# Up-projections with x's upper and lower halves in one 512-column matmul, and the two sums added on the way out

## The chip, the cores and the metric

The kernel runs on one core of a Trainium2 chip, in one launch. The metric is the device time of a run in microseconds (us), of which the median of three is given.

The engines are named as the profile names them: PE is TensorE's matmul and PEld its weight load, DVE is VectorE, ACT is ScalarE, POOL is GpSimd, SP is SyncE, which here issues the weights' DMAs. Every engine takes its instructions in the order in which they stand in its queue.

## The reference, cut to what matters

A backbone of two layers serves two groups of 128 tokens with the same weights: 256 tokens of 2048 channels. Each layer has a mixer and then a gated feed-forward network (FFN) with a convolution of width 3 over the tokens. The change is in the FFN's up-projection, here `h @ w_up` with 2048 channels in and 2 x 5632 out:

```python
def _conv_ffn(h, w_up, cw, cb, w_down, n_rows):
    bsz, n, _ = h.shape
    up = (h @ w_up).reshape(bsz, n_rows, n // n_rows, 2 * D_FF)
    pad = jnp.pad(up, ((0, 0), (0, 0), (1, 1), (0, 0)))
    conv = pad[:, :, :-2] * cw[0] + pad[:, :, 1:-1] * cw[1] + pad[:, :, 2:] * cw[2] + cb
    gate, val = jnp.split(conv.reshape(bsz, n, 2 * D_FF), 2, axis=-1)
    return (jax.nn.silu(gate) * val) @ w_down
```

All inputs are float32.

## The kernel before, in words

**Products in halves.** Each float32 operand is cut into an upper half (rounded to the matmul's fp32r) and a lower one (the rest). A product is the sum of three: upper x upper, upper weights x lower activations, lower weights x upper activations. Of the activations, `H[:, kt]` holds for each of 16 K-tiles (128 channels) the upper halves of 256 tokens in columns 0 to 255 and the lower halves in columns 256 to 511.

**Weights.** They come in units of 1 MB (`raw`, four buffers) over SP's queue, in the order of their use. Each unit is split in two steps of [128, 1024]: ACT writes the upper halves `wh` (line 149), DVE the lower ones `wl` (line 150). There are three buffers of each, so up to three steps' weights are split ahead; a step's buffer comes free when PE has used it.

**Up-projection.** A group has four output tiles of 128 channels (two of the gate, two of the values) and 16 K-tiles: eight steps of two K-tiles. `t_products` (line 789, matmuls at line 796) runs, for each output tile and K-tile, three matmuls of 256 columns, all three into the same 256 columns of a PSUM bank; two output tiles lie in a bank. A layer has 22 groups. The first (`u_products`, line 805) and the second have their own handling of the norm; the other 20 are what the change touches. Groups take their banks from the pool `acc` (four banks, line 246).

**The way out.** At a group's end (line 1396) ACT copies each bank into a buffer `z` that has a zero beside each row of tokens: one copy of the first 128 tokens of both tiles (line 1408), and one of the rest for each tile (line 1410). Then follow, piece by piece beside the next group's steps, the convolution (`conv`: line 1356 on ACT, 1360 twice on DVE), SiLU on ACT (line 1420), the product of gate and value on POOL (lines 1421 and 1424), and its split into `G` (line 702 on ACT, 703 on DVE), which the down-projection reads. CUTS (16, 16, 12) says after how many of the 44 tiles of the gate a part of the down-projection runs.

**Beside it.** The modulation vectors of later sections are spread over the stages: as units of eight matmul records on PE (line 437), or as sums along rows on DVE (line 456, four instructions a unit, `junk<-rows`). `RATES` sets how many of each go beside a unit of weights. In layer 1's FFN both run out early.

**Order.** The code queues the work in the order told; a scheduler in the recording layer then fixes the order of each engine's queue. Waits between engines are by semaphores.

Of the kernel before, what the change touches and what calls it, by code (L numbers as in the profile page):

```python
# [18 lines left out]
P = 128  # L19
D = 2048  # L20
KD = D // P
T = 256
# [36 lines left out]
# columns of the packed per-channel vectors  # L59
# [7 lines left out]
# where the output projection's 16 K-tiles lie: mixer B's first half, the heads, B's second half  # L67
# [171 lines left out]
def backbone_kernel(ctx: ExitStack, tc: tile.TileContext, a: dict):  # L239
# [6 lines left out]
    acc_pool = ctx.enter_context(tc.tile_pool(name="acc", bufs=ACC_BUFS, space=PSUM))  # L246
# [34 lines left out]
    def g0(i):  # L281
        return held["G0"][:, i]
# [4 lines left out]
    # ---- small inputs and constants  # L287
# [56 lines left out]
    # ---- modulation vectors: two rows of a tile's 32 for each condition and group of channels,  # L344
    # four K-tiles at once
# [13 lines left out]
    def mod_first(kt0, n):  # L359
        """The first norm's shift and scale of n tiles of channels."""  # L360
# [38 lines left out]
    def mod_section(s):  # L399
        """512 channels either through the array, K on partitions, or summed along rows of K."""  # L400
# [112 lines left out]
        # both kinds evenly, the products last  # L513
# [85 lines left out]
    def rsqrt_mean(sums, n, width):  # L599
        """(sums / n + eps) ** -0.5, a Newton step after the square root's table."""  # L600
# [15 lines left out]
    def spread(r):  # L616
        """Each column of r [tokens, n] on 128 columns."""
# [7 lines left out]
    def across(ps, spreads):  # L625
        """The columns as rows, the same on all partitions of ps."""
# [3 lines left out]
    def sum_tokens(x, first, last):  # L630
        """Sums over channels, tokens on partitions."""
# [37 lines left out]
    def put_norm(gain, sec=None, ahead=HL_BUFS):  # L669
        """The next norm's statistics, modulation units filling the gap in the products."""  # L670
# [28 lines left out]
    def split(out, src):  # L699
        """out[:, 0:n] the upper, out[:, n:2n] the lower halves of float32 words."""  # L700
# [25 lines left out]
    def make_folded(kt, shift):  # L726
        """Sum and difference of channels half a group apart, in their places."""
# [7 lines left out]
    def make_u(kt):  # L735
        """h before the norm's factor and the shift."""
# [22 lines left out]
    def pre_u(shift, made):  # L759
        """The statistics under way, then h itself behind the products that don't need it."""  # L760
# [14 lines left out]
    def pre_h(shift, upto=KD, made=None):  # L775
        """h's K-tiles as the first group comes to need them."""
# [28 lines left out]
    def u_products(ps, wh, wl, rhs, kts, first, last):  # L805
        """Like t_products, of the rows before the norm's factor and of the shifts; a bank for a tile."""
# [28 lines left out]
    def put_unit(ap, kt0, first, last, products, rhs, ps, end, pre=None, banks=2):  # L835
        """Four K-tiles of a group of 512 output columns, or two."""
        steps = []
        for half in range(ap.shape[-1] // 1024):
            kts = (kt0 + 2 * half, kt0 + 2 * half + 1)

            def fn(wh, wl, kts=kts):
                if kts[0] == first:
                    ps.clear()
                    ps.extend(acc() for _ in range(banks))
                products(ps, wh, wl, rhs, kts, first, last)
                if kts[1] == last:
                    end(ps)
# [19 lines left out]
    # ================================ layer 0: mixers A and B ================================  # L867
    def put_mixers():
# [18 lines left out]
        def store(out, ps, spill, func, queue=st.bg, front=False):  # L887
            """A group's sums through an activation."""
# [45 lines left out]
        def end_t(name, block, func):  # L934
            """Four channel tiles of a block, through an activation."""
# [28 lines left out]
        def queue_head(pair, hh, pt):  # L964
# [91 lines left out]
                # both directions have the same values to sum  # L1056
# [6 lines left out]
            def states():  # L1063
                """S after a direction's first chunk, and the context's after both."""
# [35 lines left out]
            def outputs():  # L1100
                """Tokens on partitions."""
# [135 lines left out]
        # as K-tiles of h come to be known, the first groups' partial sums  # L1237
# [93 lines left out]
    def open_late():  # L1331
        """Room for what comes after the mixers."""
# [397 lines left out]
```

## Time and profile before

| what | value |
|---|---|
| runs | 2369.51, 2373.82, 2376.21 us; median 2373.82 |
| profiled execution, its own time (first to last instruction: the span) | 2371.5 us |
| mean granted TensorE clock | 0.990 |
| PE, DVE, ACT, POOL busy | 98%, 70%, 49%, 16% of the span |
| HBM read | 584 MB, mean 248 GB/s |

The profiled execution has no time of its own beside the span. An engine's busy share is the union of its instructions; PE's matmuls overlap each other in the records, so a busy PE says nothing of its speed, and the distance between the starts of two matmuls does. Rows of the timeline merge neighbours with the same names: "x2" is two instructions, the time is from the first one's start to the last one's end.

### The profile page before, as it was taken

Reading aid. Unit: us, or ns where it says so; the run is one execution under the profiler, and the core shown is the slowest. Engines: PE = TensorE matmul, PEld = TensorE weight load, DVE = VectorE, ACT = ScalarE, POOL = GpSimd, SP = SyncE. Lnnn points to the kernel's source line nnn. Section 1 sums busy time; section 2 is a strip of 40 time slices with the busy share of each in tenths; the row PEclk is TensorE's granted clock in tenths of the full one; section 3 lists DMA queues with packets and bytes.
Section 4 is the critical chain, followed back from the end, with each engine's and each line's share of the span. In section 5 each row is a group of like instructions: output and inputs, shape, how many; then the busy total and the mean of one; then the engine's idle time right before and its main releaser. Section 6 shows DMA issues by size and latency. Waiting matters only on the chain.

```text
span 2371.5 us, 44833 instructions
## 1 busy us (share of the span) xinstructions
PE 2322.9 (98%) x18584; PEld 2146.4 (91%) x18584; DVE 1649.4 (70%) x2672; ACT 1170.6 (49%) x1812; POOL 373.6 (16%) x417
## 2 busy tenths in 40 slices
PE   6999999999999999999999999999999999999997
PEld 4788878788999999999999997999999999999997
DVE  3558966755777767778677787787885566555665
ACT  5336754544655534455335445546554455534552
POOL 0002321213121100111001142233110011100113
PEclk9999999999999999999999999999999999999998
DMA  8977777788667777777777778764665555555552
GB/s 322 382 311 253 262 247 276 264 313 326 228 220 298 268 289 279 292 277 287 287 288 275 287 267 311 281 213 161 231 217 190 181 179 179 193 179 180 184 176 102
DMA packets 88124, 590.11 MB, mean 249 GB/s; under 512 B 9840, under 2 KB 12272, under 8 KB 20336
## 3 DMA queue, kind: packets, MB, share of 16 engines
q1 hardware_dynamic: 84896, 582.01, 66.9%
q10 hardware_dynamic: 3024, 5.24, 0.6%
q8 instruction: 145, 2.38, 0.4%
q14 instruction: 59, 0.48, 0.1%
HBM read 584.07 MB, written 3.15 MB: 248 GB/s over the span
## 4 chain that ended last, share of the span: by engine, by line
PE 91%; DVE 4%; ACT 1%; DMA 1%; POOL 1%; issue 1%; SPq 0%; DVEq 0%; POOLq 0%; ACTq 0%
PE acc L796 77%; PE modacc L437 4%; PE acc L827 4%; DVE wl L150 1%; PE misc L1047 1%; PE modacc L382 1%; PE acc L812 1%; DVE HS L703 0%; DMA early<-in_mod 0%; DVE junk L482 0%; PE acc L1471 0%; ACT wh L149 0%; PE misc L1112 0%; DMA rows<-in_crow 0%; PE misc L1500 0%
## 5 line engine op out<-in xcount | busy, mean ns | idle before, releaser
L796 PE MATMUL acc<-HS,wh 128*128 128x256 f32 x6656 | 1227.3, 286 | 10.0 <-DVE ush L1374 4.8
L150 DVE TENSOR_TENSOR wl<-raw,wh 128x1024 fp32r<-128x1024 f32 x704 | 874.2, 1248 | 476.9 <-ACT wh L149 473.0
L149 ACT CAST wh<-raw 128x1024 fp32r<-128x1024 f32 x704 | 735.0, 1048 | 824.0 <-PE acc L796 703.5
L796 PEld LDWEIGHTS acc<-HS,wh 128*128 128x128 f32 x6656 | 1038.1, 191 | 67.9 <-issue 46.4
L796 PE MATMUL acc<-HS,wl 128*128 128x256 f32 x3328 | 944.0, 284 | 1.6 <-DVE wl L150 1.6
L796 PE MATMUL acc<-G,wh 128*128 128x256 f32 x3840 | 696.5, 284 | 0.0
L796 PEld LDWEIGHTS acc<-HS,wl 128*128 128x128 f32 x3328 | 638.7, 192 | 3.8 <-DVE wl L150 3.5
L796 PEld LDWEIGHTS acc<-G,wh 128*128 128x128 f32 x3840 | 598.1, 192 | 26.8 <-issue 22.6
L796 PE MATMUL acc<-G,wl 128*128 128x256 f32 x1920 | 543.0, 283 | 0.0
L796 PEld LDWEIGHTS acc<-G,wl 128*128 128x128 f32 x1920 | 368.2, 192 | 0.1
L1421 POOL TENSOR_TENSOR gate<-gate,c 128x128 f32<-128x128 f32 x88 | 86.6, 985 | 1126.5 <-DVE c L1360 1060.4
L456 DVE SCALAR_TENSOR_TENSOR junk<-rows 128x1024 bf16<-128x1024 f32 x176 | 222.0, 1261 | 1.4
L1360 DVE SCALAR_TENSOR_TENSOR c<-z,cw,c 128x258 f32<-128x258 f32 x352 | 171.2, 520 | 19.4 <-ACT c L1356 17.0
L437 PE MATMUL modacc<-raw,cs 128*32 128x512 f32 x832 | 114.9, 613 | 0.9 <-DMA raw<-in_mod 0.9
L1356 ACT ACTIVATE c<-z,cw 128x258 f32<-128x258 f32 x176 | 102.6, 613 | 0.0
L702 ACT CAST G<-gate 128x256 fp32r<-128x256 f32 x88 | 35.8, 407 | 129.2 <-POOL gate L1424 129.2
L827 PE MATMUL acc<-wh,HS 128*128 128x512 f32 x256 | 85.6, 402 | 0.0
L703 DVE TENSOR_TENSOR G<-gate,G 128x256 fp32r<-128x256 f32 x88 | 45.0, 511 | 53.4 <-ACT G L702 53.4
L709 POOL TENSOR_TENSOR h<-X,rstd 128x256 f32<-128x256 f32 x44 | 41.2, 946 | 245.9 <-DVE HS L703 213.1
L1303 DVE SCALAR_TENSOR_TENSOR X<-acc,mods,X 128x128 f32<-128x128 f32 x256 | 69.2, 343 | 14.9 <-PE acc L796 14.9
L593 POOL TENSOR_TENSOR sq<-X 128x256 f32<-128x256 f32 x48 | 53.3, 1110 | 154.7 <-DVE X L1303 144.7
L482 DVE SCALAR_TENSOR_TENSOR junk<-quarter,rows 128x512 bf16<-128x512 f32 x96 | 71.7, 747 | 8.5 <-ACT rows L536 5.2
(195 smaller groups left out, 1428.6 us busy)
## 6 DMA issues: line engine op xcount, KB each, us to landing
raw<-in_up SPq DMA_DIRECT2D x176, 1024.0 KB, 4.9
raw<-in_mod SPq DMA_DIRECT2D x106, 1024.0 KB, 5.3
raw<-in_down SPq DMA_DIRECT2D x88, 1024.0 KB, 4.9
raw<-in_w_in SPq DMA_DIRECT2D x49, 1024.0 KB, 6.8
rows<-in_mod SPq DMA_DIRECT2D x44, 1024.0 KB, 4.9
raw<-in_w_out SPq DMA_DIRECT2D x32, 1024.0 KB, 6.7
early<-in_mod SPq DMA_DIRECT2D x30, 1024.0 KB, 10.1
quarter<-in_modq SPq DMA_DIRECT2D x24, 512.0 KB, 3.6
```

Of the source, the lines that this page charges most:

```text
L149: nc.scalar.copy(out=wh, in_=r)
L150: self.last_split = nc.vector.tensor_tensor(out=wl, in0=r, in1=wh.bitcast(F32), op=ALU.subtract).ins
L437: nc.tensor.matmul(ps[0][32 * j : 32 * j + 32, :], lhsT=cs[:, 4 * u + j, 3 - cg : 35 - cg], rhs=raw[:, 512 * j : 512 * j + 512], start=fir ...
L456: nc.vector.scalar_tensor_tensor(out=junk, in0=raw[:, k], scalar=1.0, in1=late["rows"][:, g, k], op0=ALU.mult, op1=ALU.mult, accum_out=(mo ...
L482: nc.vector.scalar_tensor_tensor(out=junk, in0=raw[:, 512 * i : 512 * i + 512], scalar=1.0, in1=mx["rows"][:, g], op0=ALU.mult, op1=ALU.mu ...
L593: nc.gpsimd.tensor_tensor(out=sq, in0=X[:, t], in1=X[:, t], op=ALU.mult)
L796: nc.tensor.matmul(ps[b][:, jj * T : (jj + 1) * T], lhsT=w[:, i, c], rhs=rhs(kt)[:, xs], start=(kt == first and n == 0 and jj == 0), stop= ...
L827: nc.tensor.matmul(ps[g][:, :], lhsT=rhs(kt)[:, xs], rhs=w[:, i, :], start=(kt == first and n == 0), stop=(kt == last and n == 2),)
L1303: nc.vector.scalar_tensor_tensor(out=X[:, t, s], in0=z, scalar=mods[:, sec, g, t : t + 1], in1=X[:, t, s], op0=ALU.mult, op1=ALU.add,)
L1356: nc.scalar.activation(out=o, in_=z[:, 1:259], func=AF.Identity, scale=tap(w + 1), bias=tap(w + 3))
L1360: nc.vector.scalar_tensor_tensor(out=o, in0=z[:, i : i + 258], scalar=tap(w + i), in1=o, op0=ALU.mult, op1=ALU.add)
L1421: nc.gpsimd.tensor_tensor(out=y[:, 0:P], in0=sg[:, 0:P], in1=cv[j + 2][:, 0:P], op=ALU.mult)
```

## The change

For the 20 groups of each layer from the third on, a group becomes two half-groups, each of two output tiles (one of the gate, and the tile of values that belongs to it) with the whole K. A step now holds four K-tiles of 256 output columns, where it had two K-tiles of 512; the weights in HBM are laid out for it, in units of the same size. For each output tile and K-tile the new `wide_products` runs two matmuls: the upper weights on all 512 columns of `H[:, kt]`, which fills a whole bank, with the two upper-weight sums beside each other, and the lower weights on the upper 256 columns, into the bank's first half. Each output tile has a bank of its own. On the way out, ACT copies the first half's sums into `z` and DVE adds the second half's, for the first 128 tokens and then for the rest. The pool `acc` holds two pairs of banks where it held four banks, and all other users take their two banks as a pair. Convolution, gate and split are the same functions, with the tiles' numbers as arguments.

```diff
-    acc_pool = ctx.enter_context(tc.tile_pool(name="acc", bufs=ACC_BUFS, space=PSUM))
+    acc_pool = ctx.enter_context(tc.tile_pool(name="acc", bufs=ACC_BUFS // 2, space=PSUM))
...
+    def acc_pair():
+
+        return acc_pool.tile([P, 2, 512], F32, tag="acc", name="acc")
+
+    halves = []
+
     def acc():
-        return acc_pool.tile([P, 512], F32, tag="acc", name="acc")
+        if not halves:
+            pair = acc_pair()
+            halves.extend((pair[:, 0], pair[:, 1]))
+        return halves.pop(0)
...
+    def wide_products(ps, wh, wl, rhs, kts, first, last):
+
+
+        wh, wl = (w.rearrange("p k n -> p (k n)").rearrange("p (k n) -> p k n", n=256) for w in (wh, wl))
+        for j in range(2):
+            c = slice(j * P, (j + 1) * P)
+            for i, kt in enumerate(kts):
+                nc.tensor.matmul(
+                    ps[0][:, j], lhsT=wh[:, i, c], rhs=rhs(kt), start=(kt == first), stop=False,
+                    skip_group_check=True,
+                )
+                nc.tensor.matmul(
+                    ps[0][:, j, HI], lhsT=wl[:, i, c], rhs=rhs(kt)[:, HI], start=False, stop=(kt == last),
+                    skip_group_check=True,
+                )
...
+        per = 4 if products is wide_products else 2
         for half in range(ap.shape[-1] // 1024):
-            kts = (kt0 + 2 * half, kt0 + 2 * half + 1)
+            kts = tuple(range(kt0 + per * half, kt0 + per * half + per))
...
+                def end_wide(ps, i, gi=gi, tile0=tile0):
+
+                    st.flush()
+                    z = late["zs"][0]
+                    late["zs"].rotate(-1)
+                    upper, lower = (
+                        ps[0][:, :, s].rearrange("p j (r t) -> p j r t", t=64) for s in (HI, LO)
+                    )
+                    rows = z[:, :, 130:260].rearrange("p j (r t) -> p j r t", t=65)[:, :, :, 0:64]
+                    first = z[:, :, 1:129]
+                    for out, y, l in (
+                        (first, ps[0][:, :, 0:P], ps[0][:, :, T : T + P]),
+                        (rows, upper[:, :, 2:4], lower[:, :, 2:4]),
+                    ):
+                        nc.scalar.copy(out=out, in_=y)
+                        nc.vector.tensor_tensor(out=out, in0=l, in1=out, op=ALU.add)
+                    zs, cv, ft = (z[:, 0], z[:, 1]), {}, tile0 + 2 * gi + i
+                    for f in (
+                        lambda: task(cv, zs, 0, ft),
+                        lambda: task(cv, zs, 1, ft + NFT),
+                        lambda: gate(cv, 2 * gi + i, 0, 1),
+                    ):
+                        st.bg.extend((f, None))
```

**How the orders move.** ACT's queue at a group's end in layer 1, before (z is the buffer with the zeros, c the convolution, wh the upper halves of a step's weights, gate the SiLU, G what the down-projection reads):

```order
L1408 COPY z_5061<-acc 128x2x128
L1410 COPY z_5061<-acc 128x2x64 x2
L1356 ACTIVATE c<-z_5061,cw 128x258
L149 CAST wh<-raw 128x1024
L1408 COPY z_5057<-acc 128x2x128
L1410 COPY z_5057<-acc 128x2x64 x2
L1356 ACTIVATE c<-z_5057,cw 128x258
L1420 ACTIVATE gate<-c 128x258
L1356 ACTIVATE c<-z_5061,cw 128x258
L1356 ACTIVATE c<-z_5057,cw 128x258
L149 CAST wh<-raw 128x1024
```

And now, at a half-group's end in layer 1 (lines 1481, 1385, 1431 and 711 are the copies, the convolution, the SiLU and the cast to G):

```order
L149 CAST wh<-raw 128x1024 x2
L1481 COPY z_5018<-acc 128x2x128
L1481 COPY z_5018<-acc 128x2x2x64
L149 CAST wh<-raw 128x1024
L1385 ACTIVATE c<-z_5018,cw 128x258 x2
L149 CAST wh<-raw 128x1024
L1431 ACTIVATE gate<-c 128x258
L711 CAST G_2299<-gate 128x256
L149 CAST wh<-raw 128x1024 x2
```

The six copies of a group are now two for each half-group, both convolutions stand behind both copies, and the cast to G stands once in four splits.

DVE's queue at a group's end in layer 0, before (wl is a step's lower halves, junk a modulation sum):

```order
L150 TENSOR_TENSOR wl<-raw,wh 128x1024 x3
L1360 SCALAR_TENSOR_TENSOR c<-z_5061,cw,c 128x258 x2
L150 TENSOR_TENSOR wl<-raw,wh 128x1024
L1360 SCALAR_TENSOR_TENSOR c<-z_5057,cw,c 128x258 x2
L1360 SCALAR_TENSOR_TENSOR c<-z_5061,cw,c 128x258
L1360 SCALAR_TENSOR_TENSOR c<-z_5057,cw,c 128x258
L1360 SCALAR_TENSOR_TENSOR c<-z_5061,cw,c 128x258
L1360 SCALAR_TENSOR_TENSOR c<-z_5057,cw,c 128x258
L150 TENSOR_TENSOR wl<-raw,wh 128x1024
L703 TENSOR_TENSOR G_2334<-gate,G_2334 128x256 x2
L150 TENSOR_TENSOR wl<-raw,wh 128x1024
L456 SCALAR_TENSOR_TENSOR junk,mods<-rows 128x1024 x2
```

And now, at a half-group's end in layer 0 with modulation sums (line 1482 is the add, 465 a sum, 1389 the convolution, 712 the split to G):

```order
L150 TENSOR_TENSOR wl<-raw,wh 128x1024
L1482 TENSOR_TENSOR z_5014<-acc,z_5014 128x2x128
L465 SCALAR_TENSOR_TENSOR junk,mods<-rows 128x1024
L1482 TENSOR_TENSOR z_5014<-acc,z_5014 128x2x2x64
L465 SCALAR_TENSOR_TENSOR junk,mods<-rows 128x1024
L1389 SCALAR_TENSOR_TENSOR c<-z_5014,cw,c 128x258 x4
L150 TENSOR_TENSOR wl<-raw,wh 128x1024
L465 SCALAR_TENSOR_TENSOR junk,half<-rows 128x1024
L712 TENSOR_TENSOR G_2299<-gate,G_2299 128x256
L465 SCALAR_TENSOR_TENSOR junk,half<-rows 128x1024
L150 TENSOR_TENSOR wl<-raw,wh 128x1024 x2
```

Before, the two lower halves behind a group's end had only convolutions and the split to G around them; now two adds and up to four sums stand there.

## Rows read from the trace of the kernel before

**Rows 1.** The page, part 1: busy us, share, instructions by engine.

```profile
PE 2322.9 (98%) x18584; PEld 2146.4 (91%) x18584; DVE 1649.4 (70%) x2672; ACT 1170.6 (49%) x1812; POOL 373.6 (16%) x417
```

**Rows 2.** The page, part 4: the chain that ended last, by engine.

```profile
PE 91%; DVE 4%; ACT 1%; DMA 1%; POOL 1%; issue 1%; SPq 0%; DVEq 0%; POOLq 0%; ACTq 0%
```

**Rows 3.** Windows from 659 us: us, busy (x count) by engine, clock, DMA.

```profile
659.00:1120.00 461.00, 460.14 (x3766) 431.28 (x3765) 346.41 (x502) 224.46 (x362) 48.69 (x62) 1.00 0.75 278
1120.00:1590.00 470.00, 467.11 (x3818) 432.88 (x3817) 360.84 (x611) 216.27 (x340) 95.73 (x96) 1.00 0.75 278
1630.00:2360.00 730.00, 727.56 (x6041) 727.18 (x6040) 458.30 (x619) 362.36 (x559) 87.40 (x112) 1.00 0.52 183
```

**Rows 4.** Groups by line and shape: TensorE matmuls that read x's halves.

```profile
L796 PE MATMUL acc<-HS,wh 128*128 128x256 f32 x6656 | 1227.3, 286 | 10.0 <-DVE ush L1374 4.8 <-ACT HS L702 2.3 <-DVE HS L703 2.2
L796 PE MATMUL acc<-HS,wl 128*128 128x256 f32 x3328 | 944.0, 284 | 1.6 <-DVE wl L150 1.6
```

**Rows 5.** Timeline, TensorE, 1961 to 1966: start us, us, what, xcount.

```profile
1961.02 0.40 PE L796 MATMUL acc<-HS,wh 128*128 128x256 f32 x2
...
1965.72 0.41 PE L796 MATMUL acc<-HS,wh 128*128 128x256 f32 x2
```

**Rows 6.** Timeline, TensorE, 156 to 161: matmuls of 512 columns.

```profile
156.54 0.39 PE L827 MATMUL acc<-wl,HS 128*128 128x512 f32 x1
...
160.70 0.39 PE L827 MATMUL acc<-wl,HS 128*128 128x512 f32 x1
```

**Rows 7.** Timeline, TensorE, 189.4 to 190: 512 columns, then 256.

```profile
189.47 0.39 PE L827 MATMUL acc<-wh,HS 128*128 128x512 f32 x1
189.70 0.40 PE L796 MATMUL acc<-HS,wh 128*128 128x256 f32 x2
189.94 0.28 PE L796 MATMUL acc<-HS,wl 128*128 128x256 f32 x1
```

**Rows 8.** Timeline, ScalarE, layer 0: first copy behind a group.

```profile
965.78 0.38 ACT L1408 COPY z<-acc 128x256 f32<-128x256 f32 x1 [0.53 <-PE acc L796]
...
990.10 0.38 ACT L1408 COPY z<-acc 128x256 f32<-128x256 f32 x1 [0.53 <-PE acc L796]
```

**Rows 9.** Timeline, ScalarE, layer 1: first copy behind a group.

```profile
1960.49 0.38 ACT L1408 COPY z<-acc 128x256 f32<-128x256 f32 x1 [0.50 <-PE acc L796]
...
1983.63 0.38 ACT L1408 COPY z<-acc 128x256 f32<-128x256 f32 x1 [0.50 <-PE acc L796]
```

**Rows 10.** Groups by line and shape: busy us, mean ns, idle before.

```profile
L150 DVE TENSOR_TENSOR wl<-raw,wh 128x1024 fp32r<-128x1024 f32 x704 | 874.2, 1248 | 476.9 <-ACT wh L149 473.0 <-PE acc L796 2.1
L149 ACT CAST wh<-raw 128x1024 fp32r<-128x1024 f32 x704 | 735.0, 1048 | 824.0 <-PE acc L796 703.5 <-DMA raw<-in_w_in 36.8 <-DMA raw<-in_w_out 22.1
L456 DVE SCALAR_TENSOR_TENSOR junk<-rows 128x1024 bf16<-128x1024 f32 x176 | 222.0, 1261 | 1.4
L1360 DVE SCALAR_TENSOR_TENSOR c<-z,cw,c 128x258 f32<-128x258 f32 x352 | 171.2, 520 | 19.4 <-ACT c L1356 17.0
L1356 ACT ACTIVATE c<-z,cw 128x258 f32<-128x258 f32 x176 | 102.6, 613 | 0.0
L1421 POOL TENSOR_TENSOR gate<-gate,c 128x128 f32<-128x128 f32 x88 | 86.6, 985 | 1126.5 <-DVE c L1360 1060.4 <-ACT gate L1420 52.2 <-ACT wh L149 13.9
L1424 POOL TENSOR_TENSOR gate<-gate,c 128x128 f32<-128x128 f32 x88 | 57.0, 647 | 0.0
L703 DVE TENSOR_TENSOR G<-gate,G 128x256 fp32r<-128x256 f32 x88 | 45.0, 511 | 53.4 <-ACT G L702 53.4
L1410 ACT COPY z<-acc 128x128 f32<-128x128 f32 x168 | 36.8, 276 | 0.0
L702 ACT CAST G<-gate 128x256 fp32r<-128x256 f32 x88 | 35.8, 407 | 129.2 <-POOL gate L1424 129.2
L1408 ACT COPY z<-acc 128x256 f32<-128x256 f32 x84 | 31.3, 373 | 22.0 <-PE acc L796 22.0
```

**Rows 11.** Line 1372, VectorE out of PSUM: ns min/median/max.

```profile
L1372 DVE TENSOR_TENSOR uy<-acc,rstd x8: 412/418/421, 638.7 to 1615.5; 128x256 f32<-128x256 f32 x8
```

More of the change, by code (lines that the diff above doesn't have):

```diff
@@ L843, in fn @@
                     ps.clear()
-                    ps.extend(acc() for _ in range(banks))
+                    if products is wide_products:
+                        ps.append(acc_pair())
+                    else:
+                        ps.extend(acc() for _ in range(banks))
                 products(ps, wh, wl, rhs, kts, first, last)
-                if kts[1] == last:
+                if kts[-1] == last:
                     end(ps)
@@ L1394, in put_ffn, with task, gate @@
             for gi in range(nt // 2):
+                def task(cv, zs, j, ft):
+                    cv[j] = conv(zs[j], ft)
+                def gate(cv, slot, j, jv):
+                    both = late["pool"].tile([P, 516], F32, tag="gate", name="gate")
+                    sg, y = both[:, 0:260], both[:, 260:516]
+                    nc.scalar.activation(out=sg[:, 0:258], in_=cv[j][:, 0:258], func=AF.Silu)
+                    nc.gpsimd.tensor_tensor(
+                        out=y[:, 0:P], in0=sg[:, 0:P], in1=cv[jv][:, 0:P], op=ALU.mult
+                    )
+                    nc.gpsimd.tensor_tensor(
+                        out=y[:, P:T].rearrange("p (r t) -> p r t", r=2),
+                        in0=rows_of(sg, 129),
+                        in1=rows_of(cv[jv], 129),
+                        op=ALU.mult,
+                    )
+                    split(g0(slot), y)
                 def end(ps, gi=gi, tile0=tile0):
@@ L1412, in end @@
                             )
-                    def task(j):
-                        cv[j] = conv(zs[j], tile0 + 2 * gi + j % 2 + (NFT if j >= 2 else 0))
-                    def gate(j):
-                        both = late["pool"].tile([P, 516], F32, tag="gate", name="gate")
-                        sg, y = both[:, 0:260], both[:, 260:516]
-                        nc.scalar.activation(out=sg[:, 0:258], in_=cv[j][:, 0:258], func=AF.Silu)
-                        nc.gpsimd.tensor_tensor(
-                            out=y[:, 0:P], in0=sg[:, 0:P], in1=cv[j + 2][:, 0:P], op=ALU.mult
-                        )
-                        nc.gpsimd.tensor_tensor(
-                            out=y[:, P:T].rearrange("p (r t) -> p r t", r=2),
-                            in0=rows_of(sg, 129),
-                            in1=rows_of(cv[j + 2], 129),
-                            op=ALU.mult,
-                        )
-                        split(g0(2 * gi + j), y)
@@ L1432, in end @@
-                    for f, j in ((task, 0), (task, 2), (gate, 0), (task, 1), (task, 3), (gate, 1)):
-                        st.bg.extend((lambda f=f, j=j: f(j), None))
-                n = tile0 // 2 + gi
-                put_group(
-                    a["up"][layer],
-                    base_up,
-                    KD,
-                    u_products if n == 0 else t_products,
-                    hk,
-                    end,
-                    pres[n] if n < 2 else None,
-                    banks=4 if n == 0 else 2,
-                    share=BOTH if n >= SHARE_FROM else (),
-                )
+                    ft = tile0 + 2 * gi
@@ new lines, in put_ffn @@
+                n = tile0 // 2 + gi
+                if n < 2:
+                    put_group(
+                        a["up"][layer],
+                        base_up,
+                        KD,
+                        u_products if n == 0 else t_products,
+                        hk,
+                        end,
+                        pres[n],
+                        banks=4 if n == 0 else 2,
+                        share=BOTH if n >= SHARE_FROM else (),
+                    )
+                else:
+                    for i in range(2):
+                        ps = []
+                        for u in range(2):
+                            put_unit(
+                                a["up"][layer][base_up + 2 * i + u],
+                                8 * u,
+                                0,
+                                KD - 1,
+                                wide_products,
+                                hk,
+                                ps,
+                                lambda ps, i=i, end=end_wide: end(ps, i),
+                            )
+                            share_mods(BOTH)
@@ L1683, in _host @@
         order = []
-        for i in range(NFT // 2):
+        for i in range(2):
             order += [cols(0, (2 * i, 2 * i + 1)), cols(FF, (2 * i, 2 * i + 1))]
-        ups.append(units(x[f"ffn_up_{l}"], np.concatenate(order)))
+        narrow = units(x[f"ffn_up_{l}"], np.concatenate(order))
+        order = np.concatenate([np.concatenate([cols(0, (i,)), cols(FF, (i,))]) for i in range(4, NFT)])
+        ups.append(np.concatenate([narrow, units(x[f"ffn_up_{l}"], order, 8)]))
         w = x[f"ffn_down_{l}"]
```

12 lines of the change are left out of this document (9 added, 3 removed).

## The prediction

> **What bounds the kernel now.** I read the share of each engine, then the chain that ended last, then windows over the two FFN layers, then single rows of the timeline. TensorE is busy for 98% of the span, VectorE for 70% [rows 1], and the chain of waits lies on TensorE for 91% [rows 2]. In the three windows from 659 us to the end, which hold most of both FFN layers and the second mixer, TensorE is busy for 1654.8 of 1661 us, at a granted clock of 1.00, the upper of its two levels (2.4 GHz) [rows 3]. Its matmuls on x's halves waited 10.0 and 1.6 us in all [rows 4]. So the program ends when TensorE is through, and a change of the up-projections is worth what it does to the time from one matmul's start to the next, less the waits that it brings.
>
> A busy TensorE does not say how fast it goes; the starts do. In an up-projection, 39 matmuls of 256 columns lie between the first and the last row of [rows 5]: 4.70 us / 39 = 120.5 ns each, weight loads beside them. In the mixers 18 matmuls of 512 columns lie between the two rows of [rows 6]: 4.16 / 18 = 231.1 ns each. That is 9.9 ns under two of 256 columns. This difference is the whole of what the change can win.
>
> **The change, part by part.**
>
> **Matmuls.** [rows 4] have 6656 + 3328 = 9984 matmuls of 256 columns, 192 for a group of four output tiles. That is 52 groups: 10 in the mixers, 2 second groups of the FFNs, and the 40 that change (20 a layer). Each of the 40 has 64 triples (upper weights on the upper half, upper weights on the lower half, lower weights on the upper half). A triple becomes a pair: one matmul of 512 columns, one of 256. Before: 40 x 192 x 120.5 ns = 925.4 us. After: 2560 x (231.1 + 120.5) ns = 900.1 us. Gain: 25.3 us. The check on the first figure is the distance between two groups' first copies: 1983.63 - 1960.49 = 23.14 us = 192 x 120.5 ns [rows 9], with nothing lost between.
>
> The trace never has a 512-column matmul with weights standing and x moving, nor the two widths alternating for long. A matmul of 256 columns right behind one of 512 starts after 0.23 us, and the next two starts lie 0.24 us apart, 0.12 each [rows 7], so neither width seems to change the other. Bounds for the wide one: 230 ns (the 0.23 of [rows 7]) and 241 ns (twice 120.5, no gain at all), so the gain lies between 0 and 28 us. I take 231.1, the longest clean run.
>
> **The way out.** Before, ScalarE alone copied a group out: two copies of 373 ns and four of 276 ns [rows 10], 1.85 us. Now each half-group (two output tiles, a pair of banks) has two ScalarE copies of 256 elements and behind each a VectorE add out of PSUM. ScalarE has 4 x 0.373 = 1.49 us a group, 40 x 0.36 = 14 us less in all, hidden behind TensorE. VectorE has 160 adds more. The nearest row is another two-operand instruction of 256 elements out of PSUM, 0.418 us [rows 11]; the split of 256 elements in SBUF takes 511 ns [rows 10]. I take 0.42: 67 us, which brings VectorE in the three windows from 1165.6 to 1233 of 1661 us, 74%. As a sum that is hidden; the question is whether it delays the weights' lower halves, which VectorE makes and TensorE needs.
>
> **The new wait.** Copy, add, second copy and second add follow each other: the order has the second copy wait for the first add. I work through the order at a half-group's end, T = 0 at its last matmul, with means of [rows 10]. A step (a quarter of a half-group) is 8 pairs, 2.81 us. Three steps' weights are split ahead, so the step that starts at 5.62 us is split right at T: ScalarE 0.1 to 1.15, VectorE to 2.40. Behind it, as the order of layer 1 has it: copy to 1.52, add 2.40 to 2.82, copy to 3.19, add to 3.61. The next step's upper half (3.19 to 4.24) and lower half (to 5.49) are due at 8.43. Four convolution instructions of 0.52 to 7.57, then the lower half of the step due at 11.24, done at 8.82. POOL's two products (0.985 + 0.647) to 9.20 and ScalarE's cast to 9.61 hold up the step after: lower half at 11.9, due at 14.05. Everything is over 2 us early. This order has no modulation sums in it; most of layer 1 is so, and I put its cost at nothing.
>
> In layer 0 and at the start of layer 1 the order puts VectorE's modulation sums (1.26 us each) among them. The worst place has a sum between the two adds, one behind them, and two more around the split of the gate's product: adds at 2.82 and 4.50, sum to 5.76, convolution to 7.84, lower half to 9.09 (due at 8.43), sum to 10.35, gate split, sum to 12.12, lower half to 13.37 (due at 11.24): 2.1 us late. The order has this sequence, or one like it, 13 times. In 9 of them a modulation unit on TensorE lies in between, which gives 24.32 - 23.14 = 1.18 us [rows 8, 9], and 0.9 us stay. Sum: 4 x 2.1 + 9 x 0.9 = 16.5 us. The means count each instruction to its end, though the next can start a little before it, so this is an upper bound; the lower is 0, as before the change, where the lower weights made TensorE wait 1.6 us in the whole run [rows 4]. I take 9, the middle.
>
> **Banks.** The pool of four banks becomes one of two pairs. A half-group needs the pair of the half-group before last, emptied by the second add at T + 3.6 to 4.5 us and asked for at T + 11.2. The mixers and projections still take two banks at a time; there only the grain of the release is coarser. The order of the early loads on SP shifts a little with it. I take nothing for this, and 5 us either way. Weights per load and loads per group stay the same, so DMA does not change.
>
> **Sum.** 25.3 - 9 = 16.3 us, from the profiled execution's own time, 2371.5 us (the trace shows nothing around the span): 2355.2. The median of the runs is 2.3 us above that time, so the forecast is 2357.5, rounded to 2357 us.
>
> **The rivals.**
>
> **No change.** The fixed part of a matmul is small, or the wide one goes like two narrow ones, and the late lower halves eat what is left. With 241 ns for the wide one the gain is 0, and 0 to 9 us of waits come on top: 2374 to 2383. With half the gain and the same 9 us: 2373.8 - 12.7 + 9 = 2370. I give it 2372. For it: no row shows this operand pair. Against it: the run of [rows 6], if in other hands (x standing, weights moving), goes at 231 ns, and [rows 7] show no price for the change of width.
> The Trainium skill, "TensorE: Matmul & The Clock Gate", section "Wait — 56ns, not 53.3ns?", speaks for this rival: it gives start to start as the columns at 2.4 GHz plus about 2.5 ns. By that a triple would take 327.5 ns and a pair 324.9, an estimate of 6.6 us for 2560. By that rule the time stays as it is; this case's trace disagrees with it, at 120.5 and 231.1 ns with weight loads in between.
> From the rows alone, what one matmul costs beyond its columns is 2 x 120.5 - 231.1 = 9.9 ns, and so this rival has the smaller chance.
>
> **Slower.** VectorE's in-order queue becomes the bound of layer 0. The place is the end of each of its 40 half-groups, where the sums stand between the adds; the price is the 2.1 us of the worst place at each: 84 - 25.3 = 59 us more, 2432 us. It decides from 25.3 / 40 = 0.63 us a half-group. For it: VectorE is already busy for 77% of the second window [rows 3], and an add waits at the head of its queue for ScalarE. Against it: the worst sequence stands at a quarter of layer 0's places, and at most others the lower halves due soon lie ahead of the first add.
>
> **How the numbers follow.** My forecast (a gain of 7 to 30 us) has a chance of 0.77, no change 0.16, slower 0.07. The low end of the range is the whole 28 us and little waiting: 2373.8 - 30 = 2344. The high end takes in half of the no-change case: 2371. What a measurement of this kernel can tell from no change is about 0.3%, 7 us: faster means under 2366.7.
>
> **What would show it.** Matmuls of 512 columns in the up-projections starting 231 ns before the next, and a group's two half-groups 22.5 us apart in layer 1 instead of 23.14, would show the gain. Waits of TensorE's line for the lower weights on VectorE, in layer 0 alone, a few us in all, would show the price. If the 512-column starts lie 241 ns apart, the first step is wrong; if TensorE waits for VectorE or for banks by more than 25 us, the second is, and the kernel is no faster.

## The result, and the profile after

The changed kernel takes 2389.06 us (median of 4 runs, 2384.05 to 2393.06), against 2375.02 for the kernel before (four runs taken beside them): a ratio of 1.0062, 95% interval 1.0047 to 1.0077. It is slower by 0.6%. The forecast was 2357 us, and its range ended at 2371. The profiled execution has a span of 2387.1 us, 15.6 more than before, at a mean granted clock of 0.984 (0.990).

The page's shares, which answer to [rows 1], and the chain by engine, which answers to [rows 2]:

```profile
PE 2321.1 (97%) x16024; PEld 2019.0 (85%) x16024; DVE 1681.9 (70%) x2832; ACT 1169.2 (49%) x1733; POOL 391.4 (16%) x417
PE 89%; DVE 5%; DMA 2%; ACT 2%; POOL 1%; issue 1%; SPq 0%; DVEq 0%; POOLq 0%; ACTq 0%
```

TensorE has 2560 matmuls fewer and is yet busy for only 1.8 us less, and by these rounded shares the chain has left it for 2% more of the span. The list of waits says what TensorE waited for: its tile and line, the engine, tile and line waited for, us in total, times, longest. After:

```profile
...
PE acc L841 <- DVE wl L150: 9.5, 12, 1.9
PE acc L805 <- DVE ush L1403: 8.9, 2, 4.9
PE misc L637 <- DVE rd L630: 3.3, 4, 2.0
...
PE modacc L446 <- DMA raw<-in_mod: 3.1, 2, 2.7
PE misc L1069 <- POOL E L1053: 3.0, 1, 3.0
```

And before:

```profile
...
PE acc L796 <- DVE ush L1374: 4.8, 2, 3.4
...
PE misc L628 <- DVE rd L621: 2.2, 2, 2.0
...
PE acc L796 <- DVE wl L150: 1.6, 5, 0.5
PE modacc L437 <- DMA raw<-in_mod: 0.9, 1, 0.9
```

The lower halves (`wl`) are late 12 times in the new matmuls, for 9.5 us of idle time. Two waits are not in the up-projections that changed: `ush`, made by VectorE's last reads of the first group's banks, in front of an FFN's second group, grew by 4.1 us, and `E`, a product of GpSimd's for a scan in layer 0's mixers, is new.

Where the time went, by stage (us from the start of the first to that of the last matmul of a stage in each trace; "single banks" and "no sums" are experiments below):

| stage | before | after | pairs only | single banks | after, no sums | before, no sums |
|---|---|---|---|---|---|---|
| mixers, to the first out-projection | 503.1 | 511.5 | 512.0 | 499.9 | 508.6 | 501.9 |
| gap ahead of the second group, layer 0 | 1.6 | 5.2 | 5.2 | 1.6 | 5.2 | 1.6 |
| up-projections of layer 0, from the second group | 524.9 | 520.4 | 524.9 | 519.3 | 515.8 | 524.4 |
| Fourier part of layer 1's mixer and the gap ahead | 43.0 | 48.4 | 48.3 | 43.3 | 46.6 | 43.2 |
| gap ahead of the second group, layer 1 | 3.7 | 4.3 | 4.3 | 3.7 | 4.3 | 3.7 |
| layer 1, first part | 163.9 | 171.3 | 164.2 | 170.7 | 161.3 | 164.4 |
| layer 1, second and third part | 323.7 | 317.3 | 323.7 | 317.3 | 317.3 | 323.7 |
| behind the last down-projection matmul | 17.2 | 18.2 | 18.6 | 17.2 | 18.2 | 17.2 |
| span | 2371.5 | 2387.1 | 2393.1 | 2365.2 | 2369.0 | 2372.6 |

The other stages hardly differ. After less before: +8.4 +3.6 -4.5 +5.4 +0.6 +7.4 -6.4 +1.0 = +15.5 of the 15.6 us. Where neither sums nor banks disturb it, in layer 1's later parts, the change brings 6.4 us, 7.1 ns for each of their 896 pairs of matmuls; it loses ahead of the up-projections, where it changed no matmul, and at the start of layer 1. Waits are only part of the loss: up to the last down-projection matmul, TensorE's idle time grew from 35.3 to 51.9 us, and what it lost to the clock (its busy time, times one less the granted clock) from 16.7 to 29.2.

**The pairs of matmuls.** TensorE's timeline in layer 1, after (start, us, what). Between the first row and the last lie 13 pairs of a wide and a narrow matmul, 4.62 / 13 = 355 ns each, where three of [rows 5] take 361.5:

```profile
1989.86 0.39 PE L837 MATMUL acc<-HS,wh 128*128 128x512 f32 x1
1990.09 0.28 PE L841 MATMUL acc<-HS,wl 128*128 128x256 f32 x1
1990.21 0.40 PE L837 MATMUL acc<-HS,wh 128*128 128x512 f32 x1
...
1994.48 0.39 PE L837 MATMUL acc<-HS,wh 128*128 128x512 f32 x1
```

The wide matmul takes some 0.23 us, the narrow one 0.12. ScalarE's first copies behind half-groups, which answer to [rows 9], lie 11.34 us apart, 22.68 a group against 23.14 (forecast 22.5):

```profile
1982.08 0.37 ACT L1481 COPY z<-acc 128x256 f32<-128x256 f32 x1
1983.80 0.37 ACT L1481 COPY z<-acc 128x256 f32<-128x256 f32 x1 [1.35 <-DVE z L1482]
...
1993.42 0.37 ACT L1481 COPY z<-acc 128x256 f32<-128x256 f32 x1
```

**A late lower half.** VectorE at a half-group's end at the start of layer 1, and TensorE behind it:

```profile
1693.63 1.22 DVE L150 TENSOR_TENSOR wl<-raw,wh 128x1024 fp32r<-128x1024 f32 x1
1694.77 1.22 DVE L465 SCALAR_TENSOR_TENSOR junk<-rows 128x1024 bf16<-128x1024 f32 x1
1695.91 0.09 DVE L465 DVE_READ_ACCUMULATOR junk<-rows 128x1 f32 x1
1697.20 0.43 DVE L712 TENSOR_TENSOR G<-gate,G 128x256 fp32r<-128x256 f32 x1 [1.20 <-ACT G L711]
1697.55 1.22 DVE L465 SCALAR_TENSOR_TENSOR junk<-rows 128x1024 bf16<-128x1024 f32 x1
1698.69 0.09 DVE L465 DVE_READ_ACCUMULATOR junk<-rows 128x1 f32 x1
1698.69 2.36 DVE L150 TENSOR_TENSOR wl<-raw,wh 128x1024 fp32r<-128x1024 f32 x2
```

```profile
1697.67 0.40 PE L837 MATMUL acc<-HS,wh 128*128 128x512 f32 x1
1699.97 0.39 PE L841 MATMUL acc<-HS,wl 128*128 128x256 f32 x1 [1.89 <-DVE wl L150]
1700.19 0.39 PE L837 MATMUL acc<-HS,wh 128*128 128x512 f32 x1
...
1701.26 0.60 PE L837 MATMUL acc<-HS,wh 128*128 128x512 f32 x1
1701.66 0.41 PE L841 MATMUL acc<-HS,wl 128*128 128x256 f32 x1
1701.87 0.63 PE L837 MATMUL acc<-HS,wh 128*128 128x512 f32 x1
...
1704.43 0.52 PE L837 MATMUL acc<-HS,wh 128*128 128x512 f32 x1
1704.78 0.29 PE L841 MATMUL acc<-HS,wl 128*128 128x256 f32 x1
1704.91 0.40 PE L837 MATMUL acc<-HS,wh 128*128 128x512 f32 x1
```

VectorE has the sequence of the prediction's worst place: a sum, the gate's split (which waits 1.20 us for ScalarE's cast), another sum, and only then the lower half. A narrow matmul that should follow 0.23 us behind 1697.67 starts at 1699.97, 2.07 us late; 2.1 were forecast. But the wait goes on costing: from 1701.26 to 1704.43 five pairs take 3.17 us, 634 ns each where 355 is the pace. That is the lower level of the clock, and it adds 5 x 279 ns = 1.4 us to a wait of 2.1. The window from 1700 us (the third figure from the end is the granted clock):

```profile
1700.00:1705.00 5.00, 5.00 (x20) 4.35 (x21) 2.90 (x5) 1.50 (x3) 0.00 (x0) 0.66 0.94 365
```

Of the late lower halves in this part of layer 1, the clock fell behind the two longest, this one and one of 2.07 us that ended at 1762.35; behind those of 1.0 and 1.6 us it stayed at 1.00.

### The profile page after: what moved, and what is told of

It is laid out like the page before. It is cut to its first block, busy times and chain, and to the rows that moved or that the text cites. A ratio compares the mean times of both kernels' runs of the same rounds, so it can differ in the third digit from the quotient of the medians.

```text
span 2387.1 us, 39843 instructions
## 1 busy us (share of the span) xinstructions
PE 2321.1 (97%) x16024; PEld 2019.0 (85%) x16024; DVE 1681.9 (70%) x2832; ACT 1169.2 (49%) x1733; POOL 391.4 (16%) x417
## 4 chain that ended last, share of the span: by engine, by line
PE 89%; DVE 5%; DMA 2%; ACT 2%; POOL 1%; issue 1%; SPq 0%; DVEq 0%; POOLq 0%; ACTq 0%
PE acc L805 40%; PE acc L837 23%; PE acc L841 12%; PE modacc L446 4%; PE acc L852 3%; DVE wl L150 2%; PE misc L1076 1%; PE modacc L391 1%; PE acc L821 1%; DMA quarter<-in_modq 1%; DVE junk L465 1%; POOL gate L1432 1%; ACT wh L149 1%; PE acc L1543 1%; DMA raw<-in_mod 1%
## 5 line engine op out<-in xcount | busy, mean ns | idle before, releaser
L837 PE MATMUL acc<-HS,wh 128*128 128x512 f32 x2560 | 915.6, 398 | 0.0
L837 PEld LDWEIGHTS acc<-HS,wh 128*128 128x128 f32 x2560 | 483.8, 189 | 137.7 <-issue 21.8
L1432 POOL TENSOR_TENSOR gate<-gate,c 128x128 f32<-128x128 f32 x88 | 118.5, 1347 | 1215.1 <-ACT gate L1431 1110.6
L805 PE MATMUL acc<-HS,wh 128*128 128x256 f32 x1536 | 299.6, 295 | 11.7 <-DVE ush L1403 8.9
L805 PEld LDWEIGHTS acc<-HS,wh 128*128 128x128 f32 x1536 | 248.6, 198 | 42.8 <-issue 19.2
L1389 DVE SCALAR_TENSOR_TENSOR c<-z,cw,c 128x258 f32<-128x258 f32 x352 | 151.6, 486 | 6.3 <-ACT c L1385 5.7
L446 PE MATMUL modacc<-raw,cs 128*32 128x512 f32 x832 | 120.7, 614 | 3.1 <-DMA raw<-in_mod 3.1
L1481 ACT COPY z<-acc 128x256 f32<-128x256 f32 x160 | 59.3, 371 | 127.1 <-DVE z L1482 127.1
L711 ACT CAST G<-gate 128x256 fp32r<-128x256 f32 x88 | 35.8, 406 | 165.9 <-POOL gate L1435 165.8
L712 DVE TENSOR_TENSOR G<-gate,G 128x256 fp32r<-128x256 f32 x88 | 37.6, 427 | 102.0 <-ACT G L711 102.0
L1385 ACT ACTIVATE c<-z,cw 128x258 f32<-128x258 f32 x176 | 97.0, 600 | 9.7 <-DVE z L1482 8.5
## 6 DMA issues: line engine op xcount, KB each, us to landing
quarter<-in_modq SPq DMA_DIRECT2D x24, 512.0 KB, 3.6
```

What stands on the lines that cost most here:

```text
L446: nc.tensor.matmul(ps[0][32 * j : 32 * j + 32, :], lhsT=cs[:, 4 * u + j, 3 - cg : 35 - cg], rhs=raw[:, 512 * j : 512 * j + 512], start=fir ...
L805: nc.tensor.matmul(ps[b][:, jj * T : (jj + 1) * T], lhsT=w[:, i, c], rhs=rhs(kt)[:, xs], start=(kt == first and n == 0 and jj == 0), stop= ...
L837: nc.tensor.matmul(ps[0][:, j], lhsT=wh[:, i, c], rhs=rhs(kt), start=(kt == first), stop=False, skip_group_check=True,)
L1385: nc.scalar.activation(out=o, in_=z[:, 1:259], func=AF.Identity, scale=tap(w + 1), bias=tap(w + 3))
L1389: nc.vector.scalar_tensor_tensor(out=o, in0=z[:, i : i + 258], scalar=tap(w + i), in1=o, op0=ALU.mult, op1=ALU.add)
L1432: nc.gpsimd.tensor_tensor(out=y[:, 0:P], in0=sg[:, 0:P], in1=cv[jv][:, 0:P], op=ALU.mult)
```

## The experiments

**Pairs of banks alone.** The kernel before, its matmuls and copies untouched, with the changed pool:

```diff
-    acc_pool = ctx.enter_context(tc.tile_pool(name="acc", bufs=ACC_BUFS, space=PSUM))
+    acc_pool = ctx.enter_context(tc.tile_pool(name="acc", bufs=ACC_BUFS // 2, space=PSUM))
...
-        return acc_pool.tile([P, 512], F32, tag="acc", name="acc")
+        if not halves:
+            pair = acc_pool.tile([P, 2, 512], F32, tag="acc", name="acc")
+            halves.extend((pair[:, 0], pair[:, 1]))
+        return halves.pop(0)
```

> The kernel before with one part of the change alone: the pool of two pairs of banks in place of four banks; every product, copy and sum as before. Theory P (the pairs cost time outside the up-projections): about 17 us more than before, some 2391 us: 8 us more until the FFN of layer 0 begins, 4 to 5 us between the first and the second group of that FFN, 5 us around the Fourier mixer, and the 40 groups themselves at 23.1 us as before. Rival O (the pairs cost nothing by themselves; the loss outside came with the new order that the half-groups bring): 2375 us, within 4 us of before.

2394.13 us, a ratio to before of 1.0093 (1.0075 to 1.011). The pool alone costs 22 us, more than the whole loss; every row of the table that is worse in "after" ahead of layer 1's first part is about as bad here. A list of waits shows the smaller part of it: up to the last down-projection matmul TensorE is idle for 6.6 us more than before (41.9 us), and it loses 10.2 us more to the clock (26.9).

**The wide matmuls with single banks.** The changed kernel with four single banks; a half-group takes two, and copies and adds go tile by tile:

```diff
-                    ps[0][:, j], lhsT=wh[:, i, c], rhs=rhs(kt), start=(kt == first), stop=False,
+                    ps[j], lhsT=wh[:, i, c], rhs=rhs(kt), start=(kt == first), stop=False,
...
+                    for j in range(2):
+                        for out, c in ((z[:, j, 1:129], slice(0, P)), (rows_of(z[:, j], 130), slice(P, T))):
...
+                            nc.scalar.copy(out=out, in_=y)
+                            nc.vector.tensor_tensor(out=out, in0=l, in1=out, op=ALU.add)
```

> The changed kernel with the pool of four single banks: each output tile of a half-group takes its own bank and is copied out by itself, so four copies (276 ns) and four adds (344 ns) a half-group in place of two of each (371 and 420 ns). Theory P: the stretches outside the up-projections are as before (17 us off), the extra half microsecond of VectorE a half-group makes the lower halves later in layer 0 and at the start of layer 1 by 3 to 8 us: 2375 to 2380 us. Rival O: 2389 us or more, since nothing outside changes and VectorE has more to do.

2368.55 us, a ratio to before of 0.9984 (0.997 to 0.9997), 6 us under the 2375 to 2380 that were expected. The losses ahead of the up-projections are gone, mixers and all; layer 1's first part stays at 170.7 us. So they have different causes. This version beats the changed kernel by some 20 us and the kernel before barely.

**The sums left out, after and before.** Both kernels without VectorE's modulation sums, whose results stay zero:

```diff
+        nc.gpsimd.memset(mods, 0.0)
...
-                for g in range(2):
-                    row(raw, g, h)
+                pass
```

> The changed kernel without VectorE's modulation sums (that part of the computation is left out; the weights are still loaded). Theory L (sums between the adds make the weights' lower halves late, and each such wait also drops TensorE's clock): no wait of TensorE's line for a lower half over 0.3 us in the up-projections; the up-projection of layer 1's first part falls from 171.3 us to about 160, layer 0's three parts lose 4 to 5 us together. Rival: the way out by itself is too slow (copy, add, copy, add): the waits stay, and the first part of layer 1 takes 168 us or more.

> The kernel before without VectorE's modulation sums (that part of the computation is left out), as the measure for the run above. Theory L: its up-projections take what they take with the sums (layer 1's first part 163.9 us within 1 us), so the sums cost nothing in the kernel before; the half-groups of the run above then show the bare gain, 7 ns a pair (233 + 120 against 3 x 120.3): 18 us over the 40 groups. Rival: the sums cost the kernel before as much, and both runs fall by the same amount.

2371.45 and 2374.71 us, one run each. Without sums, layer 1's first part takes 161.3 us in the changed kernel, and TensorE waits for nothing there; with them 171.3. Before, they make no difference (164.4 and 163.9). The two kernels without sums also give the bare gain of the matmuls: up-projections of 524.4 + 164.4 + 323.7 = 1012.5 and 515.8 + 161.3 + 317.3 = 994.4 us, 18.1 us or 7.1 ns for each of 2560 pairs. (The clock takes 5.0 us of these stages in the changed kernel without sums and 1.7 in the other; layer 0's and layer 1's second and third parts, free of it in both, give 12.9 us for 1792 pairs, 7.2 ns.) And the sums cost the changed kernel 4.6 us in layer 0 and 10.0 in layer 1.

**The sums held back.** For two (in a third kernel three) of the four steps from a half-group's end on, no new sum is queued; all are still computed. With single banks, with pairs, and with single banks and three steps:

```diff
+                    st.hold = 2
...
-                if self.slow:
+                if self.hold:
+                    self.hold -= 1
+                elif self.slow:
                     self.next_slow()
```

> The single-bank kernel (2368.6 us, a ratio of 0.998 to before), with VectorE's modulation sums kept off the step at a half-group's end and the next one: no sum stands between the two adds any more, though in about half of the places two sums still stand ahead of the lower half after next. All the work stays in; the sums come two steps later. Theory 'late lower halves': what costs the first part of layer 1's up-projections 7 to 9 us (171 us against 164 before and 161.3 without sums) and layer 0's some 4 to 5 us is the place of the sums in VectorE's order. Then this part falls to 162 to 166 us, layer 0's three parts by 1 to 4 us together, and the time to 2356 to 2365 us. Rival 'amount': VectorE is short of time over the whole part, whatever the order; then the part stays at 170 to 172 us and the time at 2366 to 2371 us.

> The changed kernel (pairs of banks) with the same hold on the sums. Theory 'late lower halves': layer 1's first part falls from 171 to 162 to 166 us as in the single-bank kernel; the losses ahead of layer 0's up-projections (mixers 511.5 against 503.1, second group 5.2 against 1.6) stay, so 2376 to 2383 us, no faster than before. Rival 'amount': unchanged at 2386 to 2391 us. Rival 'pairs make the late halves': the pair's release is what waits for the adds, so that the hold brings more here than with single banks, and the two kernels come within 5 us of each other.

> As the single-bank kernel with the hold, but three of a half-group's four steps without a new sum instead of two; in most places both sums now stand behind the lower half after next, in about a fifth of them sums stand between the adds again, since the backlog comes out at once. Theory 'late lower halves': layer 0's parts and layer 1's first part as with the hold of two or 1 to 3 us less, 2353 to 2364 us; where the sums stand between the adds again a wait of 0.5 to 2 us returns. Rival 'amount': 2366 to 2371 us.

| | time, us | ratio to before | mixers | layer 0 | layer 1, first part |
|---|---|---|---|---|---|
| single banks | 2368.55 | 0.9984 | 499.9 | 519.3 | 170.7 |
| single banks, hold of 2 | 2365.03 | 0.997 (0.9957 to 0.9983) | 497.6 | 517.6 | 166.8 |
| single banks, hold of 3 | 2365.97 | 0.9968 (0.9955 to 0.9982) | 502.7 | 519.2 | 165.8 |
| pairs, hold of 2 | 2390.0 | 1.0073 (1.0052 to 1.0094) | 519.4 | 516.4 | 168.8 |

The profile of "single banks, hold of 2" is that kernel's fastest run (2359.55 us), that of "pairs, hold of 2" its slowest (2393.94). The matmuls on the lower halves with single banks and the hold of two (busy, mean ns, idle before it):

```profile
L835 PE MATMUL acc<-HS,wl 128*128 128x256 f32 x2560 | 724.2, 283 | 5.4 <-DVE wl L151 5.4
```

The waits fall from 9.5 to 5.4 us and layer 1's first part by 3.9, in the direction of the theory, and short of the 162 to 166 us expected: the place of the sums counts, but moving them two steps undoes under half. The 5.5 us left over the 161.3 without sums may be their place still or, by the rival, their amount: VectorE is busy for 133 of the 160 us from 1620 us on. Held for three steps, they bring no more, and the time misses the 2353 to 2364 us expected. These two are the fastest kernels here, 0.3% ahead of the kernel before. With pairs the up-projections gain 6.5 us and the time nothing, against 2376 to 2383 us expected, since the mixers' stage, with the same order up to there on TensorE, VectorE and ScalarE, took 7.9 us more in that run; the last section returns to it.

**What in the pairs costs.** In each of the four kernels above that have pairs, TensorE waits for `E` by 3.0 to 4.1 us; in none of the five with single banks. ScalarE's read of the banks on which that chain starts, and TensorE's last matmul into them, before and after:

```profile
430.33 0.60 ACT L894 ACTIVATE X<-acc 128x512 f32<-128x512 f32 x1
431.04 0.28 PE L796 MATMUL acc<-HS,wl 128*128 128x256 f32 x1
431.36 0.60 ACT L894 ACTIVATE X<-acc 128x512 f32<-128x512 f32 x1 [0.43 <-PE acc L796]
```

```profile
433.49 0.28 PE L805 MATMUL acc<-HS,wl 128*128 128x256 f32 x1
433.74 1.05 ACT L149 CAST wh<-raw 128x1024 fp32r<-128x1024 f32 x1 [2.27 <-PE acc L805]
434.80 1.28 ACT L923 ACT_TABLE_LOAD   x1
436.09 1.09 ACT L923 ACTIVATE X<-acc 128x512 f32<-128x512 f32 x2
```

Before, ScalarE reads the first bank while TensorE still writes the second (its last matmul in it starts at 431.04). After, both reads stand behind the pair's last matmul (433.49), and a weight split and the table load, which had lain beside TensorE, stand ahead of them. GpSimd's product and TensorE's first matmul on it, before and after:

```profile
442.69 1.30 POOL L1024 TENSOR_TENSOR E<-X,E 128x512 f32<-128x512 f32 x1 [0.75 <-ACT E L1019]
444.13 0.27 PE L1040 MATMUL misc<-ident,E 128*128 128x128 f32 x1
```

```profile
448.40 1.26 POOL L1053 TENSOR_TENSOR E<-X,E 128x512 f32<-128x512 f32 x1 [0.74 <-ACT E L1048]
449.72 0.33 PE L1069 MATMUL misc<-ident,E 128*128 128x128 f32 x1 [2.98 <-POOL E L1053]
```

Before, the product was done at 443.99, 0.14 us ahead of its use. With no slack there, all of the delay is paid, and more behind it. Windows of 5 us from 445 us (busy of PE, PEld, DVE, ACT, POOL, then clock and DMA), before and after:

```profile
445.00:450.00 5.00, 4.73 (x33) 3.45 (x33) 3.90 (x9) 0.75 (x2) 0.22 (x1) 0.73 0.29 100
450.00:455.00 5.00, 5.00 (x29) 3.27 (x29) 3.01 (x6) 0.78 (x1) 1.00 (x1) 0.59 0.68 243
455.00:460.00 5.00, 5.00 (x47) 4.74 (x46) 2.90 (x8) 1.51 (x3) 0.00 (x0) 1.00 0.62 216
```

```profile
445.00:450.00 5.00, 2.02 (x15) 1.56 (x13) 3.14 (x5) 2.93 (x5) 4.26 (x5) 1.00 0.42 135
450.00:455.00 5.00, 4.10 (x28) 3.03 (x27) 1.90 (x3) 1.25 (x2) 0.90 (x1) 0.70 0.21 50
455.00:460.00 5.00, 5.00 (x25) 2.92 (x26) 3.42 (x5) 0.58 (x1) 1.54 (x1) 0.50 0.54 193
460.00:465.00 5.00, 5.00 (x39) 4.74 (x38) 2.79 (x8) 1.24 (x2) 0.00 (x0) 0.78 0.73 287
```

TensorE idles for 3.9 us in the first two windows after (0.3 before), and then runs below the full clock for three windows instead of two. Two kernels undo the pair at one and at two places:

```diff
-                        ps.extend(acc() for _ in range(banks))
+                        ps.extend((acc if banks else misc)() for _ in range(banks or 2))
...
-                        banks=4 if n == 0 else 2,
+                        banks=4 if n == 0 else 0,
# the second kernel also, for the mixers' last group whose banks a sigmoid reads:
+                    elif end is last_z:
+                        ps.extend(misc() for _ in range(2))
```

> The changed kernel, but the second group of each FFN takes its two banks from another pool, one at a time, instead of a pair. Everything else stays in pairs. Theory 'grain of the release': the second group waits until the first group's second output tile is read too, because a pair comes free as a whole; with single banks TensorE's wait in front of it falls back from 4.9 us to about 1.4, the stage's gap from 5.2 to 1.6 us in layer 0 and from 4.3 to 3.7 in layer 1, and the rest stays: about 2385 us. Rival 'order alone': the gap comes from where the scheduler put the work of ScalarE and VectorE there, not from the pair; then the gap stays at 5 us.

> The same, and the last group of the mixers ahead of the second scan (ScalarE's sigmoid reads its two banks) also takes two single banks. Theory 'grain of the release': ScalarE reads the first bank before the group is over, as in the kernel before, GpSimd's products come 2 to 4 us earlier against TensorE, TensorE's wait for them (3.0 us, and some 10 us at the lower clock behind it) goes, and the stage before layer 0's out-projection falls from 511 to 519 us to 502 to 507; the time to about 2378 us. Rival 'order alone': the wait for GpSimd stays at 3 to 4 us and the stage at 508 us or more.

2389.28 us (1.0063, 1.0042 to 1.0085) and 2391.34 us (1.0072, 1.0055 to 1.0089): neither gains. The waits in front of the second group, with its banks single, and the mixers' waits with both places undone:

```profile
PE misc L805 <- DVE wl L150: 2.7, 1, 2.7
```

```profile
PE misc L1182 <- DVE oh L1176: 3.4, 2, 2.5
```

The wait named goes each time: `ush` with its 4.9 us, then `E` with its 3.0. But another comes right behind. In front of the second group the lower weights are late; gap and first part of layer 0 together stay at 178.9 us (179.0 in the changed kernel, 176.3 before). In the mixers `oh` (rows scaled by VectorE for a transpose) grows from 3.3 to 6.7 us over the run, and the stage takes 513.5 us. So both expectations failed on time: the pair makes the waits that the trace names, as taking it away at the place takes them away, but the time comes back only with single banks everywhere. The two kernels change one thing more: they take the single banks from `misc`, a pool of three banks that the scans and norms use too, so that these had fewer left. No run tells this from the order of the queues. How much of the 22 us is the pair's release and how much the order of the queues that follows from it stays open; so does the cause in the Fourier part, where no wait stands in all kernels with pairs and in none without.

## Why the prediction was wrong

**The failed step: banks.** It said of the pool: "there only the grain of the release is coarser", and "I take nothing for this, and 5 us either way". The pool by itself costs 22 us. The argument looked at the up-projections alone, where a pair does come free early enough, as I worked out; the cost lies with the other users, in the stages that the diff leaves alone, whose banks had been read one by one. A row of before could have warned me: the first matmul on `E` starts 0.14 us behind `E`, though to take that wait away by itself brought no time.

On this step the Trainium skill, "PSUM — Partial Sum Buffer", section "PSUM bank collisions raise a hardware error", has a rule that fits: guard PSUM by bank (and by quadrant of partitions). The rows of before at 430.33 and 431.04 show the gain of it, a bank read while the next is written. A tile of two banks guards by two, more than the Trainium skill's rule asks.

**The matmuls.** Right in kind, too large in size. I took 231.1 + 120.5 ns for a pair from a stage with other operands; it takes 355 in the timeline, and the stages without sums give 18.1 us instead of 25.3. The Trainium skill, "TensorE: Matmul & The Clock Gate", section "Wait — 56ns, not 53.3ns?", by which the gain would have been an estimate of 6.6 us, was further off, on the other side.

**The new wait.** The sum had 9 us for late lower halves, and the list of waits has 9.5. The mechanism and the worst single wait (2.07 against 2.1 us) were right; that the total came so near is luck, for the 9 was the middle of 0 and 16.5, and the list counts idle time alone. By the starts of the matmuls, layer 0 has eight such waits of 0.4 to 1.0 us, 4.8 us in all, and layer 1's first part six of 0.2 to 2.1 us, 7.2 in all, where my sign had them in layer 0 alone. That is 12.0 us. What I had no term for is the clock behind a wait: it fell behind two of them, for 1.4 us more in the rows from 1701.26 us and about as much behind 1762.35. Together this makes some 15 us, where the sums cost 14.6 in stages; the two agree to no better than 2 us, since the clock also falls at the start of both layers' first parts, by different amounts in the two kernels compared.

**The sum by measured terms.** -18.1 for the matmuls, +14.6 for the sums' place, and +19.1 in the other rows of the table (8.4 + 3.6 + 5.4 + 0.6 + 1.0 = 19.0, and 0.1 in small ones) make +15.6, against -16.3 forecast. Of the 31.9 us between, banks are 19, the matmuls 7, the wait 6. That the 19 are the banks' rests on the two pool experiments: in the same rows of the table the pairs alone lose 19.8 us against before, and the wide matmuls with single banks gain 2.9.

**Way out, rest of layer 1, DMA.** As forecast: layer 1's later parts run without a wait at the pace of the pairs, and the copies wait for the adds (127.1 us over the 80 second copies, 1.6 on average) with no effect on TensorE:

```profile
L1481 ACT COPY z<-acc 128x256 f32<-128x256 f32 x160 | 59.3, 371 | 127.1 <-DVE z L1482 127.1
```

**The rivals.** "Slower" came true in sign alone: its mechanism, VectorE as the bound of layer 0, did not, for layer 0's up-projections became 4.5 us shorter. The range's upper end, 2371, came from the rivals' chances and left the unknown pool at 5 us, though no row bounded it.

## What to carry to other kernels

A change of a pool touches every stage that takes from it: look for the consumers with the least slack, in the stages the diff does not name, before calling it free. A wait of TensorE costs more than its length where the clock falls behind it, and more than its idle time in the list: late operands with 9.5 us of idle time cost some 15 here. And a named wait taken away at one place need not give its time back; when the next one stands right behind it, only the version that undoes the whole cause tells its price.

## What the runs showed of the hardware that I had not expected

The clock falls behind the wait and not in it: at 1699.97 us TensorE starts again and runs at full pace for 1.3 us, and only from 1701.26 do 512-column matmuls take 0.6 us, for 3.2 us, with TensorE busy all the while. Behind the wait that ended at 1762.35 the fall came after some 0.4 us.

The spread of one kernel's runs goes with the clock. Of 23 runs of the kernel before, the fastest took 2365.24 us at a mean granted clock of 0.993, the slowest 2379.88 at 0.986. It also moves single stages. I added up, in windows of 5 us over the mixers, TensorE's idle time and its busy time times one less the granted clock. The rest is 463 to 466 us in ten of the eleven kernels, singles and pairs alike (470 with two places undone); the idle time is 24 to 26 us with single banks and 28 to 29 with pairs, and the clock takes 8 to 15 us with single banks and 14 to 26 with pairs. The changed kernel lost 19.6 us there, and with the hold, in the same order of instructions, 25.8: this stage's figure from one profile is uncertain by some 6 us for that reason alone, and the 8.4 us of the mixers are sure only because five kernels with single banks (498 to 503 us) and six with pairs (509 to 519) do not overlap.
